# A transformer block's feed-forward part: source order on every engine, another load order for one weight sum, other final scalings on GpSimd

## The chip, the cores and the metric

The kernel runs on one core of a Trainium2 chip. Its time is the device time of one execution in microseconds (us); lower is better. Times come from runs of the whole kernel; everything about the inside of it comes from one profiled execution.

## The reference

One block of a model with a sequence of 512 tokens, width 2048 and a feed-forward width of 5632, everything in float32:

```python
u = rmsnorm(h, attn_norm_w)
z, xbc, dt_raw, q, kc, vc, ks, vs, kw, vw, gate_raw = split(u @ w_in)
y_ssd = ssd_mixer(...)            # a chunked state-space mixer
y_att = nsa_mixer(...)            # compressed, selected and window attention
h = h + concatenate([y_ssd, y_att]) @ w_out
v = rmsnorm(h, ffn_norm_w)
h = h + (silu(v @ w_gate) * (v @ w_up)) @ w_down
return rmsnorm(h, final_norm_w)
```

The change touches the last three lines: the feed-forward part and the final norm.

## The kernel before, in words

Up to about 900 us the kernel does the input projection, both mixers and the output projection. From there on it multiplies by the feed-forward weights. A product of two float32 matrices is made of three matmuls on halves of the numbers: each operand is split into a high part (ScalarE, `a_hi`, L117) and a low part (VectorE, `lo`, L120), and the matmuls are high x high, high x low (L1119, L1120) and low x high (L1121). The third matmul of each group of three is thus the first that needs the low part of a weight.

The gate and up products use a scheme with seven products in place of eight (Strassen and Winograd). A weight block of 1024 x 256 is cut into four quarters 11, 12, 21, 22; from them come the sums S1 = 21 + 22 and S3 = 21 + 11. The seven products are done in the order M1, M2, M6, M7, M5, M3, M4. M1 takes quarter 11, M2 quarter 12, M6 the quarter 11 with S1 added to it, M7 takes S3, M5 takes S1, M3 takes 12 with 11 added to it, M4 takes 22. One product is one *step* of 24 matmuls (128 x 256 each). The 22 *units* have two *sides* each, first gate, then up, so that a unit has 14 steps; the first and the last unit alternate their sides at the start (`pair_at_once`).

Weights come in buffers called `F`. The list `loads` sets the order of the blocks of a side: "11 12 S1 S3 22". A plain quarter is one load on SyncE's queue (L1065). S1 and S3 are two transfers: a load of one quarter (SyncE, L1065), and then a second transfer issued by GpSimd (L1067), which adds the other quarter onto it in the buffer and can only start when the first has landed. A side's five blocks pass through seven buffers, and a load is issued when a buffer comes free. Each weight block is then prepared for its step: where a sum is wanted, VectorE adds two buffers (`add`, L126, F<-F); ScalarE makes the high part three steps ahead of the product, VectorE the low part two steps ahead, both into buffers called `R`. VectorE and ScalarE also empty the results of the products (L126 with `ps`, L1288, L1291, L1278), VectorE multiplies (`mul`, L123) by the norm's row `rrow` and by the gate, and one transfer of 1792 KB per unit, issued by ScalarE (L1329), stores the unit's result in HBM (`g_d`).

From about 1950 us the down projection follows in the same scheme, in 36 visits of seven steps with 3 to 6 pairs of weight tiles each, and at the end the final norm: sums of squares, a power (`rst`, L1502, GpSimd), a row of factors, and sixteen multiplications of 128 x 512 in two halves, `lo_h` and `hi_h`, each followed by its stores (L1521).

The order in which the source emits all this is fixed by `run_step` and by a list of background tasks that advance by one after each group of three matmuls. In the kernel before, however, that isn't the order on the engines: the whole body is under a scheduler, which simulates the program and gives every engine (SyncE's and GpSimd's queues too) an order of its own.

Of the kernel before, what the change touches and what calls it, by code (L numbers as in the profile page):

```python
# [15 lines left out]
KD = D // 128  # L16
# [91 lines left out]
def body(ctx, tc, xT, w_in, w_out, w_gate, w_up, w_down, w1k, w1v, cols, rows, kst, out):  # L108
    nc = tc.nc
    act, dve, pool, pe = nc.scalar, nc.vector, nc.gpsimd, nc.tensor  # L110
    sch = Sched()
# [814 lines left out]
    order = [U_DTG]  # L926
# [113 lines left out]
    loads, items, steps = [], [], []  # L1040
# [46 lines left out]
    def prep(upto):  # L1087

        form(upto)
        while nxt["item"] <= min(upto, len(items) - 1):  # L1090
            i = nxt["item"]
            form(i + 1)
            b = items[i][0]
            hl[i].append(hl_place(b))
            assert hl[i][1] is not None, (i, hz.busy)
            lo(dve, hz.ap(hl[i][1], b.n), b.ap(), hz.ap(hl[i][0], b.n))
            b.read()
            nxt["item"] += 1
            advance()
# [8 lines left out]
    def run_step(s):  # L1108
        feed(s.i)
        if s.before:  # L1110
            s.before()
        prep(s.i + 2)
        n = s.blk.n
        ats = hl.pop(s.i)
        h, l = [hz.ap(a, n) for a in ats]
        p, q = s.psum()
        for k in range(s.blk.n):
            ah, al = s.rhs(k)
            pe.matmul(q, h[:, k, :], ah, start=(k == 0), stop=False)  # L1119
            pe.matmul(q, h[:, k, :], al, start=False, stop=False)  # L1120
            pe.matmul(q, l[:, k, :], ah, start=False, stop=(k == s.blk.n - 1))  # L1121
            sch.tick()
        for a in ats:
            hz.free(a, n)
        if s.after:
            s.after(p)
# [111 lines left out]
                     M5: (q["S1"], None), M3: (q["12"], q["11"]), M4: (q["22"], None)}  # L1238
        return q

    def add_loads(q, order="11 12 S1 S3 22"):
        loads.extend(q[a] for a in order.split())

    turn_ = {"n": 0}
# [5 lines left out]
    def banks(which=BANK):  # L1250
        got = {}

        def get(p):
            def g():
                b, h = which[p]
                if b not in got:
                    got[b] = bank()
                return got[b], got[b][:, 256 * h:256 * h + 256]
            return g
        return get  # L1260

    def v_rhs(p):
        a = V_OF[p]
        if a == 0:
            return lambda k: (P2["V0"][:, k, 0, :], P2["V0"][:, k, 1, :])
        if a < 3:
            return lambda k: (P2["VV"][:, a - 1, k, 0, :], P2["VV"][:, a - 1, k, 1, :])
        return lambda k: (P2["T"][a - 3][:, k, 0, :], P2["T"][a - 3][:, k, 1, :])
# [3 lines left out]
    def gu_after(u, side):  # L1272

        def after(pr):
            def ev(p):
                p1 = P2["HH"][:, 2 + side, :]
                if pr == M1:
                    act.activation(p1, p[:, lo_h], AF.Copy)  # L1278
                    return
                ct = P2["CT"].rearrange("p (s c a) t -> p s c (a t)", s=2, c=2)  # L1280
                c = ct[:, side].rearrange("p a t -> p (a t)")
                g = ct[:, 0].rearrange("p a t -> p (a t)")
                c11, c12, c21, c22 = [c[:, 256 * i:256 * i + 256] for i in range(4)]
                if pr == M6:
                    add(dve, c[:, 0:512].rearrange("p (a t) -> p a t", a=2), p.rearrange("p (a t) -> p a t", a=2),
                        p1[:, None, :].to_broadcast([128, 2, 256]))
                elif pr == M7:
                    dve.tensor_tensor(c21, p[:, lo_h], c12, ALU.subtract)  # L1288
                elif pr == M5:
                    add(dve, c22, p[:, lo_h], c21)  # L1290
                    dve.tensor_tensor(c12, c12, p[:, lo_h], ALU.subtract)  # L1291
                elif pr == M4:
                    add(dve, c[:, 256:768], p, c[:, 256:768])
                    if side == 0:
                        rr = rrow[:, None, :].to_broadcast([128, 2, 512])
                        c2 = ct[:, 0]
                        mul(dve, c2, c2, rr)
                        act.activation(g, g, AF.Silu)
                        sch.add(times_r(c2, rr))
                    else:  # L1300
                        mul(dve, c, c, g)
                        sch.add(g_forms(u))
            return ev
        return after
# [56 lines left out]
    def step_r3(ev):  # L1361
        def after(p):
            next(r3, None)
            ev(p)
        return after

    qs = {}
# [2 lines left out]
            qs[u, side] = quad(w[u], 0, 8)  # L1370
    def pair_at_once(u, before=None):

        loads.extend(qs[u, side][a] for a, side in (("11", 0), ("11", 1), ("12", 0), ("12", 1), ("S1", 0), ("S3", 0),
                                                    ("22", 0), ("S1", 1), ("S3", 1), ("22", 1)))
        seq = [(0, M1), (1, M1), (0, M2), (1, M2)] + [(i, p) for i in range(2) for p in SEQ[2:]]
        af = {0: gu_after(u, 0), 1: gu_after(u, 1)}
        bk = {0: banks(), 1: banks()}
        for n, (side, p) in enumerate(seq):
            ev = af[side](p)
            if u == 0 and n in (1, 2):  # L1380
                ev = step_r3(ev)
            b, plus = qs[u, side]["form"][p]
            s = Step(b, v_rhs(p), bk[side](p), after=ev, before=start_ff(n) if u == 0 and n < 3 else None, plus=plus)
            if u == NP - 1:
                done[V_SLOT.index(V_OF[p]) - GRING] = s.i
# [20 lines left out]
    def feed(i):  # L1406

        n = len(G)
        if n < NP and done.get(n - GRING, i) + 2 <= i:
            if n == NP - 1:  # L1410
                sch.run_until(("g", n))
            G[n] = P2["slot"][n % GRING][:, 0:7]
            nc.scalar.dma_start(f(G[n]), g_d[n])
        if "H0" not in P2 and len(G) > 0 and not any(fz.busy[NZ2:]):
            load_h(0)
            load_h(1)
            P2["H0"] = True
# [90 lines left out]
            pe.transpose(p[:, i * 128:(i + 1) * 128], rst[:, 4 + b + i:5 + b + i].to_broadcast([128, 128]), ident)  # L1508
        act.activation(rrow[:, t], p[:, 0:256], AF.Copy)

    def half_out(a, js):

        t = (lo_h, hi_h)[a]
        p = P2["rp", t.start // 128]
        for j in js:
            h = out_rows(j)[:, :, t]
            if j % 3 == 1:
                mul(pool, h, h, rrow[:, None, t].to_broadcast([128, 2, 256]))
            else:
                mul(dve, h, h, p[:, None, 0:256].to_broadcast([128, 2, 256]))  # L1520
            (nc.sync, nc.scalar)[j % 2].dma_start(out[2 * j:2 * j + 2, :, t].rearrange("c p t -> p c t"), h)  # L1521

    def d_end(j):
        order = [i for i in range(NJ) if i != j] + [j]

        def after(pr):
            def ev(p):
                H = P2["H"][j]
                q = p[:, 0:256]
                if pr == M1:  # L1530
                    d_add(j, M1, p, False, True)
                elif pr == M7:
                    add(dve, H[:, 3:5, :], p[:, None, lo_h].to_broadcast([128, 2, 256]), H[:, 3:5, :])
                elif pr == M5:
                    add(dve, H[:, 4, :], q, H[:, 4, :])
                    dve.tensor_tensor(H[:, 2, :], H[:, 2, :], q, ALU.subtract)
                    half_sum(lo_h)
                elif pr == M6:
                    add(dve, H[:, 0, :], q, H[:, 0, :])
                    add_x(j)  # L1540
                elif pr == M2:
                    add(dve, H[:, 1, :], q, H[:, 1, :])
                elif pr == M4:
                    add(dve, H[:, 3, :], q, H[:, 3, :])
                    half_sq(j, 0)
                elif pr == M3:
                    half_row(lo_h)
                    add(dve, H[:, 2, :], q, H[:, 2, :])
                    half_sq(j, 1)
                    half_out(0, order[:2])  # L1550
                    half_sum(hi_h)
                    half_out(0, order[2:5])
                    half_row(hi_h)
                    half_out(0, order[5:])
                    half_out(1, order)
            return ev
        return after

# [5 lines left out]
    for v, (j, a, b) in enumerate(visits):  # L1564
        q = quad(w_down[j], a, b, by_dma=False, s3_by_pool=v < 6)
# [9 lines left out]
        for n, p in enumerate(SEQ_END if end else SEQ_D):  # L1575
            blk, plus = q["form"][p]
            s = Step(blk, g_rhs(p, a), (lambda: (lambda t: (t, t[:, 0:256]))(bank())) if end else bk(p), after=af(p),
                     before=down_before(v) if n == 1 and 1 <= v < NJ - 1 else None, plus=plus)
        done.update((i, s.i) for i in range(a, b))

    def run_rest():
        pre_oa()
        for s in steps:
            run_step(s)
        sch.drain()
        for n in ("tt", "vv", "ws"):
            close_pool(n)

# [145 lines left out]
```

## Time and profile before

| | |
|---|---|
| three runs | 2479.65, 2484.35, 2484.87 us (median 2484.35) |
| the profiled execution | 2476.37 us, of which the span is 2473.9 us |
| mean granted TensorE clock | 0.952 |
| TensorE busy | 2259.7 us, 91% of the span |
| VectorE busy | 1802.3 us, 73% |
| ScalarE busy | 1096.1 us, 44% |
| GpSimd busy | 434.9 us, 18% |
| moved by DMA | 419.18 MB, mean 169 GB/s |

Busy time of TensorE includes the stretches in which its granted clock was half, so 91% busy doesn't say that 91% of the span was used at full speed. All stages share these means; the feed-forward part has to be read by windows of its own.

### The profile page before, as it was taken

What the parts mean: (1) busy time and instruction counts of PE and PEld (TensorE: products, weight loads), DVE (VectorE), ACT (ScalarE), POOL (GpSimd) and SP (SyncE); (2) the same over time, 40 slices, a digit from 0 to 9 for tenths busy, and PEclk for the clock granted to TensorE, in tenths of its full rate; (3) what the DMA queues carried; (4) which work ended last, traced back from release to release, by engine and by line L of the source; (5) the groups of instructions that cost most, each with busy time, mean ns of one, the idle gap of its engine ahead of it and who ended that gap; (6) DMA issues with size and microseconds to landing.
All of it is one profiled execution on the core that took longest, in us unless ns stands there. A gap on an engine that the chain in (4) does not pass through costs nothing. (4 is left out here: it accounts for less than half of the span.)

```text
span 2473.9 us, 39809 instructions
## 1 busy us (share of the span) xinstructions
PE 2259.7 (91%) x15376; PEld 2095.7 (85%) x15376; DVE 1802.3 (73%) x2916; ACT 1096.1 (44%) x1767; POOL 434.9 (18%) x441
## 2 busy tenths in 40 slices
PE   7999999999898999898988888788989889999987
PEld 5888888888687789888988888788989889999987
DVE  7699666777986677666676767576666777788886
ACT  4454446666765444333343333333333333333353
POOL 1011341332232330000000000000000121112122
PEclk9999999999999999998999899999989999899998
DMA  4222432222243767576767566666766857686865
GB/s 166 90 73 69 157 107 91 80 70 81 69 147 103 240 178 205 168 207 187 201 169 218 168 191 184 203 185 181 207 181 195 300 209 253 181 280 166 297 158 162
DMA packets 135469, 419.18 MB, mean 169 GB/s; under 512 B 16448, under 2 KB 22096, under 8 KB 129648
## 3 DMA queue, kind: packets, MB, share of 16 engines
q1 hardware_dynamic: 99840, 251.91, 31.1%
q0 software_dynamic: 25776, 77.70, 15.6%
q10 hardware_dynamic: 9664, 87.04, 8.7%
q8 instruction: 120, 1.97, 0.3%
q14 instruction: 69, 0.57, 0.1%
HBM read 354.45 MB, written 58.20 MB: 167 GB/s over the span
## 5 line engine op out<-in xcount | busy, mean ns | idle before, releaser
L117 ACT ACTIVATE R<-F 128x1024 fp32r<-128x1024 f32 (+4 forms) x576 | 512.1, 910 | 871.2 <-DVE F L126 421.7
L120 DVE TENSOR_TENSOR R<-F,R 128x1024 fp32r<-128x1024 f32 (+4 forms) x576 | 617.4, 1081 | 45.8 <-ACT R L117 31.2
L126 DVE TENSOR_TENSOR F<-F 128x1024 f32<-128x1024 f32 (+4 forms) x168 | 170.9, 1017 | 280.7 <-DMA F<-in_w_up 196.3
L224 PE MATMUL ps_g<-u_hi,whi 128*128 128x512 f32 x592 | 238.2, 402 | 0.0
L226 PE MATMUL ps_g<-u_hi,wlo 128*128 128x512 f32 x592 | 236.6, 400 | 0.0
L225 PE MATMUL ps_g<-u_lo,whi 128*128 128x512 f32 x592 | 236.2, 399 | 0.0
L1119 PE MATMUL ps_g<-T,R 128*128 128x256 f32 x704 | 201.5, 286 | 5.3 <-ACT R L117 5.3
L120 DVE TENSOR_TENSOR wlo<-wraw,whi 128x512 fp32r<-128x512 f32 x196 | 153.0, 783 | 70.9 <-ACT whi L117 70.0
L1119 PE MATMUL ps_s<-T,R 128*128 128x256 f32 x698 | 199.8, 286 | 4.1 <-ACT R L117 4.1
L1121 PE MATMUL ps_s<-T,R 128*128 128x256 f32 x698 | 200.1, 287 | 3.6 <-DVE R L120 3.6
L1121 PE MATMUL ps_g<-T,R 128*128 128x256 f32 x704 | 201.4, 286 | 1.0 <-DVE R L120 1.0
L1120 PE MATMUL ps_g<-T,R 128*128 128x256 f32 x704 | 200.8, 285 | 1.5 <-DVE T L120 1.5
L1119 PE MATMUL ps_t<-T,R 128*128 128x256 f32 x678 | 194.7, 287 | 6.3 <-ACT R L117 6.3
L1120 PE MATMUL ps_s<-T,R 128*128 128x256 f32 x698 | 199.2, 285 | 0.0
L1121 PE MATMUL ps_t<-T,R 128*128 128x256 f32 x678 | 194.9, 287 | 3.9 <-DVE R L120 3.9
L1120 PE MATMUL ps_t<-T,R 128*128 128x256 f32 x678 | 194.0, 286 | 0.0
L117 ACT ACTIVATE whi<-wraw 128x512 fp32r<-128x512 f32 x196 | 122.6, 626 | 145.2 <-PE ps_g L225 95.5
L1121 PE MATMUL ps_g<-VV,R 128*128 128x256 f32 x354 | 107.6, 304 | 42.3 <-DVE R L120 42.3
L1121 PE MATMUL ps_s<-VV,R 128*128 128x256 f32 x367 | 111.0, 303 | 37.6 <-DVE R L120 37.6
L1119 PEld LDWEIGHTS ps_g<-T,R 128*128 128x128 f32 x704 | 135.8, 193 | 6.6 <-ACT R L117 6.5
L1119 PEld LDWEIGHTS ps_s<-T,R 128*128 128x128 f32 x698 | 135.0, 193 | 4.8 <-ACT R L117 4.8
L1121 PEld LDWEIGHTS ps_s<-T,R 128*128 128x128 f32 x698 | 134.4, 193 | 5.1 <-DVE R L120 4.8
(406 smaller groups left out, 6495.0 us busy)
## 6 DMA issues: line engine op xcount, KB each, us to landing
F<-in_w_gate SPq DMA_DIRECT2D x110, 512.0 KB, 7.0
F<-in_w_up SPq DMA_DIRECT2D x110, 512.0 KB, 6.1
wraw<-in_w_in SPq DMA_DIRECT2D x164, 256.0 KB, 3.0
g_d<-F ACTq DMA_DIRECT2D x22, 1792.0 KB, 13.6
F<-in_w_gate POOLq DMA_DIRECT2D x44, 512.0 KB, 8.9
F<-in_w_up POOLq DMA_DIRECT2D x44, 512.0 KB, 11.2
F<-in_w_down SPq DMA_DIRECT2D x68, 320.0 KB, 3.7
T<-g_d ACTq DMA_DIRECT2D x12, 1792.0 KB, 10.9
```

What stands on the lines that cost most here:

```text
L117: act.activation(dst, src, AF.Copy, scale=scale)
L120: eng.tensor_tensor(dst, src, f(hi), ALU.subtract)
L126: eng.tensor_tensor(o, a, b, ALU.add)
L224: pe.matmul(p, hi_t[i][:, j, :], ah, start=(k == 0), stop=False)
L225: pe.matmul(p, hi_t[i][:, j, :], al, start=False, stop=False)
L226: pe.matmul(p, lo_t[i][:, j, :], ah, start=False, stop=(k == u.nk - 1))
L1119: pe.matmul(q, h[:, k, :], ah, start=(k == 0), stop=False)
L1120: pe.matmul(q, h[:, k, :], al, start=False, stop=False)
L1121: pe.matmul(q, l[:, k, :], ah, start=False, stop=(k == s.blk.n - 1))
```

## The change

It has three parts.

1. The steps after the first `KD` (those of the output projection) are put in a region of manual schedule. In it every engine runs in the order in which the source emits its instructions.
2. The load order of a side becomes "11 S1 12 S3 22": S1 is loaded second rather than third. In `pair_at_once` the up side's quarter 12 goes behind the gate side's S1.
3. In the final norm GpSimd takes the fourth and the seventh of each half's eight multiplications instead of the three with j % 3 == 1.

```diff
-    def add_loads(q, order="11 12 S1 S3 22"):
+    def add_loads(q, order="11 S1 12 S3 22"):
         loads.extend(q[a] for a in order.split())
...
-        loads.extend(qs[u, side][a] for a, side in (("11", 0), ("11", 1), ("12", 0), ("12", 1), ("S1", 0), ("S3", 0),
+        loads.extend(qs[u, side][a] for a, side in (("11", 0), ("11", 1), ("12", 0), ("S1", 0), ("12", 1), ("S3", 0),
                                                     ("22", 0), ("S1", 1), ("S3", 1), ("22", 1)))
...
-    def half_out(a, js):
+    def half_out(a, js, order):
...
-            if j % 3 == 1:
+            if order.index(j) in (3, 6):
                 mul(pool, h, h, rrow[:, None, t].to_broadcast([128, 2, 256]))
             else:
                 mul(dve, h, h, p[:, None, 0:256].to_broadcast([128, 2, 256]))
...
-                    half_out(0, order[:2])
+                    half_out(0, order[:2], order)
                     half_sum(hi_h)
-                    half_out(0, order[2:5])
+                    half_out(0, order[2:5], order)
                     half_row(hi_h)
-                    half_out(0, order[5:])
-                    half_out(1, order)
+                    half_out(0, order[5:], order)
+                    half_out(1, order, order)
...
-        for s in steps:
+        for s in steps[:KD]:
             run_step(s)
-        sch.drain()
+        with tc.manual_schedule():
+            for s in steps[KD:]:
+                run_step(s)
+            sch.drain()
```

Where instructions stand on the engines is seen in the built programs. On GpSimd, the two accumulating transfers of each side in the middle of the gate and up stage, before. `DMASW` are the semaphores of GpSimd's transfers, and each of these rows waits for the earlier use of its own one; `DMAHW` are those of the transfers of the other queues, here that of the load onto which the row accumulates. By the addresses in the program the first of each pair is S3's, the second S1's:

```order
L1067 DMA F<-in_w_gate 128x1024 [waits DMAHW6_49,DMASW6_49]
L1067 DMA F<-in_w_gate 128x1024 [waits DMAHW7_49,DMASW7_49]
L1067 DMA F<-in_w_up 128x1024 [waits DMAHW3_49,DMASW0_49]
L1067 DMA F<-in_w_up 128x1024 [waits DMAHW4_49,DMASW1_49]
L1067 DMA F<-in_w_gate 128x1024 [waits DMAHW1_49,DMASW2_49]
L1067 DMA F<-in_w_gate 128x1024 [waits DMAHW2_49,DMASW3_49]
```

The same rows of GpSimd after; here the first of each pair is S1's:

```order
L1067 DMA F<-in_w_gate 128x1024 [waits DMAHW4_49,DMASW6_49]
L1067 DMA F<-in_w_gate 128x1024 [waits DMAHW6_49,DMASW7_49]
L1067 DMA F<-in_w_up 128x1024 [waits DMAHW1_49,DMASW0_49]
L1067 DMA F<-in_w_up 128x1024 [waits DMAHW4_49,DMASW1_49]
L1067 DMA F<-in_w_gate 128x1024 [waits DMAHW7_49,DMASW2_49]
L1067 DMA F<-in_w_gate 128x1024 [waits DMAHW1_49,DMASW3_49]
```

Before, the two loads below a pair stand next to each other on SyncE (neighbouring semaphores); after, other transfers are issued between them.

On VectorE, the start of an up side before. The row with a `DMASW` wait and F<-F is the sum for M6; behind it stands a low part (R<-F,R), that of M2, and the row that waits for `DMASW0` further down is the low part of M7:

```order
L120 TENSOR_TENSOR R<-F,R 128x1024 [waits DMAHW5_49,PE_49,Activation_49]
L126 TENSOR_TENSOR F<-ps_g,F 128x256 [waits DVE_49]
L1291 TENSOR_TENSOR F<-F,ps_g 128x256
L126 TENSOR_TENSOR F<-F 128x1024 [waits DMASW1_49,DVE_49]
L120 TENSOR_TENSOR R<-F,R 128x1024 [waits DMAHW6_49,PE_49,Activation_49]
L126 TENSOR_TENSOR F<-F 128x1024 [waits DVE_49]
L126 TENSOR_TENSOR F<-ps_s,F 128x512 [waits PE_49]
L120 TENSOR_TENSOR R<-F,R 128x1024 [waits Activation_49]
L123 TENSOR_TENSOR F<-F,rrow 128x1024 [waits DVE_49]
L120 TENSOR_TENSOR R<-F,R 128x1024 [waits DMASW0_49,PE_49,Activation_49]
```

The same place after:

```order
L120 TENSOR_TENSOR R<-F,R 128x1024 [waits DMAHW4_49,Activation_49]
L126 TENSOR_TENSOR F<-F 128x1024 [waits DMASW0_49,DVE_49]
L120 TENSOR_TENSOR R<-F,R 128x1024 [waits DMAHW7_49,PE_49,Activation_49]
L126 TENSOR_TENSOR F<-ps_s,F 128x512 [waits PE_49]
L123 TENSOR_TENSOR F<-F,rrow 128x1024 [waits DVE_49]
L120 TENSOR_TENSOR R<-F,R 128x1024 [waits Activation_49]
L123 TENSOR_TENSOR F<-F,rrow 128x1024 [waits Activation_49]
L120 TENSOR_TENSOR R<-F,R 128x1024 [waits DMASW1_49,PE_49,Activation_49]
L126 TENSOR_TENSOR F<-F 128x1024
```

The sum for M6 now waits for the first of GpSimd's pair instead of the second, the low part of M7 for the second instead of the first, and the sum for M3 stands seven rows behind that for M6 instead of two.

At the end of the program, GpSimd's rows before:

```order
L1502 TENSOR_TENSOR rst<-rst,nhalf 128x2 [waits DVE_49]
L123 TENSOR_TENSOR F<-F,rrow 128x2x256 [waits DMASW6_49,Activation_49]
L123 TENSOR_TENSOR F<-F,rrow 128x2x256 x2
L1502 TENSOR_TENSOR rst<-rst,nhalf 128x2 [waits DVE_49]
L123 TENSOR_TENSOR F<-F,rrow 128x2x256 [waits Activation_49]
L123 TENSOR_TENSOR F<-F,rrow 128x2x256 x2
```

and after:

```order
L1502 TENSOR_TENSOR rst<-rst,nhalf 128x2 [waits DVE_49] x2
L123 TENSOR_TENSOR F<-F,rrow 128x2x256 [waits DMASW7_49,Activation_49]
L123 TENSOR_TENSOR F<-F,rrow 128x2x256
L123 TENSOR_TENSOR F<-F,rrow 128x2x256 [waits Activation_49]
L123 TENSOR_TENSOR F<-F,rrow 128x2x256
```

The second power now stands directly behind the first instead of behind three multiplications, and each half has two multiplications here instead of three.

## The prediction

> **What bounds the kernel now.** I first looked at the stretches of the span, to see which stage has something to lose. Columns: stretch, its length, then busy time (and instructions) of PE, PEld, DVE, ACT and POOL, the granted TensorE clock, the DMA engines' share, GB/s.
>
> ```profile
> 1100.00:1900.00 800.00, 700.75 (x5528) 696.47 (x5527) 534.59 (x612) 291.92 (x329) 57.13 (x66) 0.92 0.66 191
> ...
> 1900.00:2000.00 100.00, 84.35 (x644) 81.64 (x642) 69.08 (x91) 34.53 (x48) 13.52 (x10) 0.92 0.84 295
> 2000.00:2100.00 100.00, 96.58 (x798) 96.16 (x798) 80.48 (x110) 38.91 (x57) 21.49 (x14) 0.98 0.60 199
> 2100.00:2200.00 100.00, 95.11 (x741) 94.00 (x742) 80.69 (x114) 36.53 (x52) 20.47 (x17) 0.92 0.72 213
> 2200.00:2300.00 100.00, 97.69 (x805) 95.94 (x804) 81.07 (x115) 39.22 (x55) 19.11 (x15) 1.00 0.73 223
> ```
>
> The first row is the steady gate and up stage: TensorE is idle for 99 us of 800 and its clock is 0.92. The last row, in the down projection, shows that TensorE can be 98% busy at a clock of 1.00. Which wait ends last in the steady stage is told by its waits (total, times, longest) and by the matmuls that read `VV`, the operand of M2:
>
> ```profile
> ACT R L117 <- DVE F L126: 288.8, 30, 13.5
> DVE F L126 <- DMA F<-in_w_up: 162.8, 17, 10.2
> DVE F L126 <- DMA F<-in_w_gate: 54.4, 16, 4.9
> ```
>
> ```profile
>   DVE R L120: 99.2, 19
> ```
>
> All of TensorE's waits there are for a low part of M2, 99.2 us, and VectorE waits 162.8 us for a transfer into an up side's buffer. One unit's timeline joins the two (start, length, what, idle time before it):
>
> ```profile
> 1437.14 5.66 SPq L1065 DMA_DIRECT2D F<-in_w_up  x3
> ...
> 1441.22 0.86 POOL L1067 DMA_DIRECT2D F<-in_w_up  x1 [17.73 <-DMA F<-in_w_up]
> 1443.75 0.86 POOL L1067 DMA_DIRECT2D F<-in_w_up  x1 [1.67 <-DMA F<-in_w_up]
> ...
> 1445.12 0.33 ACTq L1329 DMA_DIRECT2D g_d<-F  x1
> ...
> 1448.67 0.41 DVE L1291 TENSOR_TENSOR F<-F,ps_g 128x256 f32<-128x256 f32 x1
> 1459.00 1.23 DVE L126 TENSOR_TENSOR F<-F 128x1024 f32<-128x1024 f32 x1 [9.92 <-DMA F<-in_w_up]
> 1460.15 1.22 DVE L120 TENSOR_TENSOR R<-F,R 128x1024 fp32r<-128x1024 f32 x1
> ...
> 1460.32 2.95 ACT L117 ACTIVATE R<-F 128x1024 fp32r<-128x1024 f32 x3 [12.93 <-DVE F L126]
> ...
> 1461.42 0.58 PE L1121 MATMUL ps_g<-VV,R 128*128 128x256 f32 x1 [6.26 <-DVE R L120]
> 1461.80 0.41 PE L1119 MATMUL ps_g<-VV,R 128*128 128x256 f32 x1
> 1462.01 0.41 PE L1120 MATMUL ps_g<-VV,R 128*128 128x256 f32 x1
> ```
>
> The second row of POOL is S1's accumulate. It is issued at 1443.75 and releases VectorE at 1459.00, 15.25 us later, with the `g_d` store in flight beside it. VectorE stands at M6's sum for 9.92 us; the low part of M2, which needs none of S1, is queued behind it, and TensorE waits 6.26 us for that. After the wait the matmuls start 0.21 us apart. Elsewhere they start 0.118 us apart, and a shorter wait brings the slow pace too:
>
> ```profile
> 1985.56 0.58 PE L1121 MATMUL ps_s<-V,R 128*128 128x256 f32 x1 [2.79 <-DVE R L120]
> ...
> 1990.42 0.39 PE L1121 MATMUL ps_t<-V,R 128*128 128x256 f32 x1
> ...
> 1991.01 0.28 PE L1119 MATMUL ps_t<-T,R 128*128 128x256 f32 x1
> ...
> 1993.96 0.28 PE L1119 MATMUL ps_g<-T,R 128*128 128x256 f32 x1
> ```
>
> (From 1991.01 to 1993.96 are 25 matmuls, 0.118 us each.) The length of a unit comes from its store:
>
> ```profile
> L1329 ACTq DMA_DIRECT2D g_d<-F x22: 326/326/338, 961.2 to 1983.1; - x22
> ...
> DMA to landing us min/median/max: 10.5/13.6/17.2
> ```
>
> (1983.1 - 961.2)/21 = 48.66 us per unit. Its 14 x 24 = 336 matmuls need 336 x 0.118 = 39.65. Of the 9.0 us between, 99.2/(800/48.66) = 6.0 are the wait and 3.0 the half clock behind it with small change.
>
> **The change part by part.**
>
> *S1 earlier, and really in the listed place.* Before, S1 was third in the list, but GpSimd's rows show S3 issued ahead of it. After, its load takes the buffer that is freed about nine steps before the sum that needs it; before it was five. Nine steps are 9 x 24 x 0.118 = 25.5 us. Before, from the first of the three load issues to the landing were 1459.0 - 1437.14 = 21.9 us; the three issues lie within 5.66 us and S1's is the second, so its own way took about 20. Both are below 25.5: S1's stall goes, worth up to 9.0 us a unit.
>
> What is late next is S3, which now takes the crowded place beside the store. Its product M7 comes eight steps after its load's issue: 8 x 24 x 0.118 = 22.7 us, less the high part (1.0 us) and the low part (1.22 us) ahead of it, 20.4 us. Its transfers there are bounded by the gate side of the same stage from below (its longest wait for DMA is 4.9 us against 10.2, so about 5 us shorter: 15 us, no stall) and by S1's 20.0 to 21.9 us from above. At a denser pace these may stretch: DMA share 0.66 at 48.66 us is 0.79 at 40.7; stretched in that ratio, 20.0 becomes 23.9, 3.5 us too late. I take the value nearest to the row of the same place, 20.0 to 21.9 against 20.4: about 0.8 us of stall, and with it a part of the half clock, 1.2 of the 3.0 us. A unit becomes 39.65 + 2.0 = 41.65, a gain of 7.0; over the 20 units in which the sides follow each other, **-140 us** (ends: -20 x 9.0 = -180 and, with 3.5 us of stall and 3.0 of clock, -20 x 2.5 = -50).
>
> [...]
>
> *Quarter 12 third instead of second.* Its high part is needed four steps after its issue, its product seven (19.9 us on TensorE). Plain loads in this stage have no row above S1's two in sequence, 20 us, and the plain half of that is 1441.22 - 1437.14 = 4.1 us: hidden, cost 0. If the cover goes, ScalarE stands at it, and with it every later high part.
>
> *Strict order in gate and up.* VectorE is busy 534.59/800 x 48.66 = 32.5 us a unit, 82% of 39.65; ScalarE 17.8, 45%. Both still fit, and the sum for M3 no longer stands ahead of an evacuation. At a unit's end a multiplication (1.22) and three subtractions (0.69, 0.42 and 0.42 in the rows of that time, 2.75 us in all) stand in one piece ahead of a low part that has a lead of two steps, 5.7 us: hidden. Unit 0 and the last unit alternate sides and their up side still loads S1 eighth of ten: no gain credited there, and in unit 0 the splitting of the operands (`T`), which VectorE now does in line, is ahead of low parts: **+5 us** (four `lo` of 1.22 us or longer; ends 0 and +10).
>
> *Strict order at the change of stages and in the down projection.* Before, the scheduler mixed the end of the last unit with the first visits; from 1900 to 2000 TensorE is busy 84.35 us at 0.92. In strict order this can be worse or better by what it loses now, 100 - 84.35 + 8 of clock = 24 us: I take **+4**. From 2000 on TensorE is above 95% busy with VectorE at 81 of 100; there are seven matmuls to one VectorE instruction (805 to 115). Strict order can win what the row 2100 to 2200 lacks against 2200 to 2300 (64 matmuls x 0.118 = 7.6 us) or lose as much again in each of four such stretches, 30 us: I take 0.
>
> *The final scalings.* The tail before:
>
> ```profile
> 2458.17 3.08 DVE L123 TENSOR_TENSOR F<-F,ps_v 128x512 f32<-128x512 f32 x5 [0.89 <-ACT rrow L1509]
> 2461.16 0.15 DVE L1501 TENSOR_SCALAR rst<-ps_m 128x2 f32<-128x2 f32 x1
> 2463.78 3.08 DVE L123 TENSOR_TENSOR F<-F,ps_m 128x512 f32<-128x512 f32 x5 [2.46 <-ACT rrow L1509]
> ...
> 2458.21 3.71 POOL L123 TENSOR_TENSOR F<-F,rrow 128x512 f32<-128x512 f32 x3 [1.07 <-ACT rrow L1509]
> 2461.89 0.69 POOL L1502 TENSOR_TENSOR rst<-rst,nhalf 128x2 f32<-128x2 f32 x1
> 2463.82 3.71 POOL L123 TENSOR_TENSOR F<-F,rrow 128x512 f32<-128x512 f32 x3 [1.24 <-ACT rrow L1509]
> ```
>
> The second power waits for three multiplications, until 2461.89; after, it stands ahead of them, and the second half starts when VectorE is through with six of the first, 6 x 0.62 + 0.15 = 3.9 after 2458.17: 2462.0 instead of 2463.8, 1.7 us. Each half's last multiplication on GpSimd falls from 3.71 to 2 x 1.24 = 2.5, VectorE's grows from 3.08 to 3.7, the same end. With earlier stores: **-3 us** (ends -4 and 0).
>
> Sum: -140 + 5 + 4 + 0 - 3 = -134 us. Against the profiled execution (2476.37) that is 2342. The three runs lie 3.3 to 8.5 us above that execution, and their median is 2484.35; against it the sum gives **2350 us**.
>
> **The rivals.**
>
> *The whole stall goes* (12 in 100). S3 lands in time like the gate side's transfers, and a unit is 39.65: -180 + 6, 2310 us. For it: most waits for in_w_gate were short. Against: the store lies beside S3.
>
> *S3 takes S1's place* (18 in 100). If the two transfers stretch with density, a unit of P us has a stall of 20.0 x 48.66/P - 20.4 and P is 39.65 + stall + 3.0. P settles at 44.25 with a stall of 1.6: -20 x 4.4 + 6, 2402 us; with 21.9 in place of 20.0 it settles at 45.6 with 3.0, 2429 us. VectorE would then stand at the low part of M7. For it: the 15.25 us beside the store. [...]
>
> *Strict order ruins the down projection* (6 in 100), the other side. Its 455 us have TensorE busy 95% now by a scheduler's order; with evacuations standing ahead of low parts on VectorE, TensorE and VectorE could take turns. At a share x the stage takes 0.95 x 455/x; it decides against the change when that is 134 us more, x below 0.73. At 0.70 it is +162, 2512 us. For it: VectorE's 81 of 100 leaves little room. Against: the low parts have two steps of lead.
>
> *The change doesn't do what it says* (4 in 100): the sum for M6 is late for another reason than its place, since the accumulate itself took 15 of the 20 us. A load issued ten us earlier would have to be slower by as much; then 2484 us.
>
> **How the numbers follow.** The forecast, 60 in 100: 2350, its own range 2315 to 2385 (the ends of the small terms and stalls of 0 to 2 us). The range 2300 to 2430 takes in the first rival and the second. A measurement of this kernel tells about 0.2% from no change. Faster: 0.60 + 0.12 + 0.17 = 0.89; slower: the third and a half of the fourth, 0.08; same 0.03.
>
> **What would show it.** Right: no wait of VectorE for in_w_up at L126 above 2 us, the `g_d` stores 41 to 42 us apart, the clock of the steady stage at 0.97 or more, DMA share near 0.78. The second rival shows as waits of ACT L117 or DVE L120 for DMA F<-in_w_up and stores 44 to 46 us apart. The third shows as PE under 90 in the hundred-us windows of the down projection. The power of the second half should start within 4 us of the first. The prediction is wrong above all if M2 waits again, or if the steady gain is given back behind the last store.

## The result and the profile after

The changed kernel takes 2321.31 us (median of four runs, 2318.81 to 2321.64) against 2482.0 us (the three runs of the table before and a fourth, 2471.6 to 2484.87): a ratio of 0.9357, 95% interval 0.9328 to 0.9387. The forecast was 2350 us, faster, with a range of 2300 to 2430.

Its profiled execution took 2321.24 us, span 2319.3. The stretches after, with the same columns as before:

```profile
1000.00:1780.00 780.00, 779.52 (x6545) 779.31 (x6545) 637.45 (x717) 347.28 (x390) 65.66 (x76) 1.00 0.79 232
1780.00:1818.00 38.00, 25.01 (x183) 24.30 (x182) 23.59 (x31) 11.02 (x16) 6.30 (x6) 0.85 0.77 271
1818.00:1868.00 50.00, 44.30 (x348) 43.77 (x348) 39.69 (x58) 18.07 (x29) 11.35 (x6) 0.94 0.65 250
1868.00:1968.00 100.00, 91.82 (x747) 91.22 (x746) 72.48 (x107) 35.88 (x53) 18.30 (x14) 0.95 0.72 239
1968.00:2068.00 100.00, 95.55 (x786) 95.04 (x785) 84.58 (x124) 38.66 (x57) 19.19 (x16) 0.97 0.77 240
```

For 780 us in the gate and up stage TensorE is idle for half a microsecond and has its full clock; before, it was idle 99 of 800 us at 0.92. In this stage TensorE is now what bounds the time. What is left of waits lies in the last unit (second row) and in the down projection (last three). The units' stores and their landing:

```profile
L1329 ACTq DMA_DIRECT2D g_d<-F x22: 326/326/356, 963.9 to 1820.1; - x22
...
DMA to landing us min/median/max: 6.7/6.7/19.1
```

A steady unit takes 40.0 us, where the matmuls alone need 39.65. The store lands in 6.7 us (median) instead of 13.6. The span is 154.6 us shorter, and the starts of the stores divide this: up to the first store nothing is won (+2.7 us), from first to last the 21 intervals give -165.7, from the last store to the end of the last weight product the down projection takes 481.6 us instead of 472.3 (+9.3), and the tail behind that product 17.6 instead of 18.6 (-1.0). The timeline of one store, in the place in which S1 stood before:

```profile
1324.09 0.33 ACTq L1329 DMA_DIRECT2D g_d<-F  x1
...
1325.27 2.90 SPq L1065 DMA_DIRECT2D F<-in_w_up  x3
...
1333.99 0.86 POOL L1067 DMA_DIRECT2D F<-in_w_up  x1 [14.29 <-DMA F<-in_w_up]
1337.80 0.86 POOL L1067 DMA_DIRECT2D F<-in_w_gate  x1 [2.95 <-DMA F<-in_w_gate]
```

Only one accumulating transfer of this side (S3's, 1333.99) now lies behind the store; S1's was issued 15 us earlier, at 1318.8, and lands as the store starts. The store itself lands at 1331.1, before S3's is issued. The up side's accumulating transfers land after 5.5 us here (median), so that S3 is there some 14 us after the load at 1325.27, where the prediction had taken 20 to 22 against a need of 20.4.

### The profile page after: what moved, and what is told of

Its sections match the earlier page's. It is cut to its first block, busy times and chain, and to the rows that moved or that the text cites. A ratio compares the mean times of both kernels' runs of the same rounds, so it can differ in the third digit from the quotient of the medians.

```text
span 2319.3 us, 39808 instructions
## 1 busy us (share of the span) xinstructions
PE 2215.3 (96%) x15376; PEld 2057.3 (89%) x15376; DVE 1803.0 (78%) x2918; ACT 1098.1 (47%) x1767; POOL 430.9 (19%) x439
## 5 line engine op out<-in xcount | busy, mean ns | idle before, releaser
L120 DVE TENSOR_TENSOR R<-F,R 128x1024 fp32r<-128x1024 f32 (+4 forms) x576 | 610.6, 1067 | 37.8 <-ACT R L117 28.2
L1121 PE MATMUL ps_s<-T,R 128*128 128x256 f32 x698 | 203.0, 291 | 23.0 <-DVE R L120 23.0
L1119 PE MATMUL ps_s<-T,R 128*128 128x256 f32 x698 | 201.2, 288 | 0.0
L1120 PE MATMUL ps_s<-T,R 128*128 128x256 f32 x698 | 201.1, 288 | 0.0
L1121 PE MATMUL ps_t<-T,R 128*128 128x256 f32 x678 | 192.6, 284 | 0.4 <-DVE R L120 0.4
L1120 PE MATMUL ps_t<-T,R 128*128 128x256 f32 x678 | 192.0, 283 | 0.0
L1119 PE MATMUL ps_t<-T,R 128*128 128x256 f32 x678 | 192.0, 283 | 0.0
L1121 PEld LDWEIGHTS ps_s<-T,R 128*128 128x128 f32 x698 | 136.7, 196 | 25.3 <-DVE R L120 25.1
L1119 PEld LDWEIGHTS ps_s<-T,R 128*128 128x128 f32 x698 | 136.7, 196 | 0.0
L1120 PEld LDWEIGHTS ps_s<-T,R 128*128 128x128 f32 x698 | 136.6, 196 | 0.0
L1121 PEld LDWEIGHTS ps_g<-T,R 128*128 128x128 f32 x704 | 133.8, 190 | 3.0 <-DVE R L120 2.9
L1119 PEld LDWEIGHTS ps_g<-T,R 128*128 128x128 f32 x704 | 133.6, 190 | 1.7 <-ACT R L117 1.3
```

Source lines behind the costliest of these rows:

```text
L120: eng.tensor_tensor(dst, src, f(hi), ALU.subtract)
```

## The experiments

All are timed against the kernel before on the chip on which they ran. These chips differ: the kernel before has a median of 2480 us on one and 2499 on two others, so kernels of different sets are compared by ratios, and kernels of one set by times. Ratios don't carry from chip to chip exactly either: the kernel after has 0.9357 above and 0.9291 when timed again below, at nearly the same time, 2321 and 2322 us. A difference of under 0.7% between sets therefore tells nothing.

**Each part alone.** The manual region with the old lists and old scalings (the edit is against the kernel after):

```diff
-    def add_loads(q, order="11 S1 12 S3 22"):
+    def add_loads(q, order="11 12 S1 S3 22"):
...
-                                    (("11", 0), ("11", 1), ("12", 0), ("S1", 0), ("12", 1), ("S3", 0),
+                                    (("11", 0), ("11", 1), ("12", 0), ("12", 1), ("S1", 0), ("S3", 0),
...
-            if order.index(j) in (3, 6):
+            if j % 3 == 1:
```

> The manual region alone: old load order, old last scalings. Source order puts S1's transfers ahead of S3's on both queues, but S1 is still third in the list, so that its load is issued about 5 steps (14.2 us) before the sum that needs it. Theory (the place of S1's load decides): its way is 13.8 us in the quiet place of the profile after and 20 us beside the store, so the stall shrinks but stays, 1 to 5 us a unit with half clock behind it: 2360 to 2430 us, stores 41.5 to 45 us apart. Rival (only the order of the two accumulating transfers counts, or the strict order as such): no wait for in_w_up, stores 40 us apart, 2325 us.

Measured: 2459.96 us, ratio 0.9928 (0.9904 to 0.9952). The direction is the theory's, the size isn't: 2360 to 2430 was expected. The other half, the two lists alone in the kernel before, without a manual region:

> The load order alone: the scheduler still sets the order on every engine, old last scalings. In the built program S1's accumulate now stands ahead of S3's, but the two loads are still neighbours. Theory (place of S1's load decides): S1 comes at the time at which S3 came before, about 10 us sooner than before; the wait of 6 us at M6's sum goes for the most part, 2340 to 2400 us. Rival (strict order is what brings the gain): the stall stays at 5 to 6 us a unit, about 2480 us.

Measured: 2312.55 us, ratio 0.933 (0.930 to 0.9359): the whole gain. Again on another chip, beside the kernel after:

> The kernel after once more, beside the next two on the same chip, since the chips differ by more than the kernels do. Theory (with the new load order the strict order costs some 10 us, in the last unit and the down projection): ratio to before 0.935 to 0.938. Rival (strict order costs nothing): equal to the next kernel's ratio within 0.002.

> The load order alone, under the scheduler, beside the kernel after. Theory: ratio 0.003 to 0.006 below the kernel after's (7 to 14 us). Rival: within 0.002 of it.

Measured: the kernel after 2322.34 us, ratio 0.9291 (0.9267 to 0.9316); the load order alone 2309.64 us, 0.9253 (0.9223 to 0.9284). So the load order alone brings all of it. It has the lowest median of the study; the medians lie 12.7 us apart and the profiled spans 16.1 (2322.1 and 2306.0 us), so that the region of manual schedule, with the new scalings, seems to cost 13 to 16 us on top of it. That isn't clear of the noise: the intervals overlap, and one of the five runs of the load order alone took 2323.75 us. The steady stage of the load order alone, and what GpSimd issues there in a unit:

```profile
1000.00:1760.00 760.00, 760.00 (x6384) 760.00 (x6383) 621.66 (x703) 345.00 (x381) 63.93 (x74) 1.00 0.79 231
```

```profile
1425.42 0.86 POOL L1067 DMA_DIRECT2D F<-in_w_up  x1 [9.87 <-DMA F<-in_w_up]
1433.00 0.86 POOL L1067 DMA_DIRECT2D F<-in_w_up  x1 [6.72 <-DMA F<-in_w_up]
```

The two transfers stand 7.6 us apart under the scheduler, 2.5 us in the kernel before. The scheduler itself puts S1 first once the list does; no manual region is needed for it.

**S1 behind S3, in strict order.**

```diff
-    def add_loads(q, order="11 S1 12 S3 22"):
+    def add_loads(q, order="11 12 S3 S1 22"):
```

> The kernel after with the load order 11 12 S3 S1 22 for the steady units: strict order, but S3's transfers ahead of S1's, as the scheduler had them before. Theory: S1 is the second of two accumulating transfers that start within 3 us of each other beside the store; the stall of about 6 us a unit returns with the half clock, stores 47 to 49 us apart, 2450 to 2480 us. Rival (the strict order on VectorE hides it): under 2350 us.

Measured: 2595.23 us, ratio 1.0474 (1.0443 to 1.0504): worse than before, and outside what was expected. TensorE waits twice a unit, 6 us on the up side and 2 on the gate side, and the stores stand (2080.4 - 965.5)/21 = 53.1 us apart. By the source, S1's load now waits for one buffer more than in the kernel before, where the scheduler had only put it behind S3 in the queues. The region alone, above, is in strict order too and has S1 third: there TensorE waits 3.7 us a unit on the up side and not at all on the gate side, here 6.2 and 2.2. One place later in the list thus costs about one step of 24 matmuls (2.8 us at full pace) on either side. In strict order the wait on the up side goes 0, 3.7, 6.2 us with S1 second, third and fourth.

**Does the store lengthen S1's way?** In the manual region with the old lists the store was issued later, once by 22 us (out of the way) and once by 9 us (beside the two accumulating transfers, as in the kernel before):

```diff
-        yield 6
+        yield 68      # the other one: 31
         nc.scalar.dma_start(g_d[u], f(sg))
```

> The manual region with the old load order, and each unit's store to HBM (1792 KB) issued some 22 us later, out of the way of the up side's loads. In manual_only S1's way from load issue to landing was 17 us on the up side with the store just ahead of it, its load alone 6.8 to 8.5 us against 3.5 to 5 on the gate side, and TensorE waited 3.8 us a unit. Theory (the store sets the length of that way): the way falls to 14 to 15 us, TensorE's wait to 0 to 1.5 us a unit, 2370 to 2410 us. Rival (two accumulating transfers at once are what is long, the store counts little): the way stays above 16 us, 2445 to 2470 us.

> The manual region with the old load order and each unit's store issued some 9 us later than in source order, so that it is in flight beside the up side's two accumulating transfers, as it was in the kernel before. Theory (the store and two accumulating transfers at once make the 15 us): S1's accumulate takes 13 to 15 us instead of 8.7, its way 18 to 20 us, TensorE's wait 5 to 6.5 us instead of 3.8; ratio to before 1.00 to 1.02 against 0.993. Rival (the store counts little): accumulate under 11 us, ratio 0.985 to 0.997.

Times: 2451.92 us, 0.982 (0.9793 to 0.9847), with the store out of the way, and 2486.58 us, 0.9942 (0.9917 to 0.9966), with it beside. Both lie in the range of their rival; what the transfers do is another matter. The transfers in the steady stage (KB each, median us to landing), first the region alone, then the store beside, then out of the way:

```profile
g_d<-F ACTq DMA_DIRECT2D x12, 1792.0 KB, 6.7
F<-in_w_up POOLq DMA_DIRECT2D x26, 512.0 KB, 8.6
```

```profile
g_d<-F ACTq DMA_DIRECT2D x13, 1792.0 KB, 12.5
F<-in_w_up POOLq DMA_DIRECT2D x26, 512.0 KB, 12.9
```

```profile
g_d<-F ACTq DMA_DIRECT2D x13, 1792.0 KB, 10.6
F<-in_w_up POOLq DMA_DIRECT2D x26, 512.0 KB, 9.3
```

Beside two accumulating transfers the store takes 12.5 us instead of 6.7, and they take 12.9 instead of 8.6; in the kernel after, one at a time, they take 5.5 (median of the up side). That is the collision of the kernel before, made again. TensorE's wait went up with it, 57.6/12 = 4.8 us against 48.4/13 = 3.7. The signs are the theory's, the sizes fall short of it.

Moving the store away did not bring the expected 0 to 1.5 us a unit. TensorE's waits at M2 in 600 us of the steady stage, for the region alone and then for the store out of the way:

```profile
  DVE R L120: 48.4, 13
```

```profile
  DVE R L120: 51.8, 26
```

They are twice as many and half as long, 2.0 us: the store now lies beside the gate side's transfers, and M2 waits on both sides. VectorE's waits for M6's sum tell the sides apart (total, times, longest), again for the region alone and then for the store out of the way:

```profile
DVE F L126 <- DMA F<-in_w_up: 105.6, 13, 8.9
DVE F L126 <- DMA F<-in_w_gate: 39.8, 13, 4.3
```

```profile
DVE F L126 <- DMA F<-in_w_gate: 85.5, 12, 8.4
DVE F L126 <- DMA F<-in_w_up: 72.7, 13, 6.3
```

On the up side, which the store left, a wait falls from 8.1 to 5.6 us; on the gate side, to which it came, one rises from 3.1 to 7.1. From the issue of its load to its landing S1 takes 13.3 us on the up side instead of 15.7 (medians), and TensorE waits there for about 1.3 us a unit instead of 3.7; on the gate side it takes 15.1 us instead of 13.0, and TensorE waits for 2.7 us instead of not at all. So the theory holds for the side that the store leaves, and what was won there was lost on the other. Of the 3.7 us the store accounts for about two thirds; the rest stays without it, at 5 steps of lead. The steady stage as a whole won next to nothing: the stores are (1976.4 - 987.2)/21 = 47.1 us apart against (1949.2 - 958.1)/21 = 47.2, although TensorE's mean clock over the profiled run is 0.97 instead of 0.96. Why the better clock doesn't show there is open, and so is the 1% between the two ratios, which come from two chips.

**The down projection under the scheduler.**

```diff
         with tc.manual_schedule():
-            for s in steps[KD:]:
+            for s in steps[KD:KD + 14 * NP]:
                 run_step(s)
-            sch.drain()
+        for s in steps[KD + 14 * NP:]:
+            run_step(s)
+        sch.drain()
```

> The kernel after with the down projection left to the scheduler; the gate and up steps stay in the manual region. From the last store to TensorE's end were 472 us before and 482 us after. Theory A (strict order costs the down projection about 9 us): 472 us again, 2312 us in all. Theory B (the five waits of 2 to 8 us there come from stored units' loads of 1792 KB that share the DMA engines with the weights, whatever the order): 478 to 484 us, 2317 to 2325 us.

Measured: 2321.79 us (2310.85 to 2328.2), ratio 0.9376 (0.9342 to 0.9409). The time lies in theory B's range. In the profile, the fastest of its runs, the down projection took 469.6 us from the last store to the end of the last weight product, as theory A has it, but the last unit grew by 5 us, and the median doesn't tell it from the kernel after. Inconclusive.

**S1 sooner in the last unit.** What stops TensorE at the end of the gate and up stage in the kernel after:

```profile
1784.91 0.86 POOL L1067 DMA_DIRECT2D F<-in_w_up  x1 [3.65 <-DMA F<-in_w_up]
...
1788.62 1.23 DVE L126 TENSOR_TENSOR F<-F 128x1024 f32<-128x1024 f32 x1 [12.96 <-DMA F<-in_w_up]
1789.76 1.22 DVE L120 TENSOR_TENSOR R<-F,R 128x1024 fp32r<-128x1024 f32 x1
...
1791.03 0.58 PE L1121 MATMUL ps_s<-T,R 128*128 128x256 f32 x1 [9.90 <-DVE R L120]
```

It is the old chain once more, in the unit in which S1 is still the eighth load. The edit makes it the seventh:

```diff
-    ("S3", 0), ("22", 0), ("S1", 1), ("S3", 1), ("22", 1)
+    ("S3", 0), ("S1", 1), ("22", 0), ("S3", 1), ("22", 1)
```

> The kernel after, with the up side's S1 of the first and last unit loaded before the gate side's 22 instead of behind it (seventh of ten instead of eighth). Theory (the waits of 4.2 us at 937 and 9.9 us at 1791 are the sum for M6 of the up side waiting for an S1 that is loaded too late, the same mechanism as in the steady units before): both go, with their half clock -14 to -20 us, 2301 to 2308 us. Rival (the next item, S3 or 22, is late instead): 2315 to 2325 us.

> The same edit on the kernel whose down projection is left to the scheduler. Theory (the two gains add): 2290 to 2300 us by the profile. Rival (the scheduler was hiding the late S1 of the last unit in part, or the down projection loses again what the last unit wins): 2305 to 2320 us.

> The load order alone, under the scheduler, with the same edit. There TensorE had no wait over 1.5 us before 1775, and the last unit took 9.7 us longer than a steady one, 4.9 of it a wait for a high part. Theory (that wait is not S1's): no change beyond 5 us, 2305 to 2315 us. Rival (S1 is late there too and the scheduler fills the time with other work): 2295 to 2303 us.

> The kernel after with the up side's S1 of the first and last unit loaded seventh, beside the kernel after. On another chip both of its waits at those places were gone and the last store came 11 us sooner, but the whole did not show it. Theory (that chip's down projection was slower): ratio 0.003 to 0.006 below the kernel after's, like the load order alone. Rival (the down projection gives the 11 us back, its waits moving with the start): within 0.002 of the kernel after.

Measured: 2336.75 us, 0.9364 (0.9341 to 0.9386) on the kernel after; 2332.22, 0.9341 (0.9315 to 0.9367) with the down projection scheduled; 2325.28, 0.9317 (0.9292 to 0.9342) on the load order alone. Beside the kernel after on one chip it was 2339.84 us against 2322.34, 0.9366 (0.9342 to 0.9391) against 0.9291 (0.9267 to 0.9316): slower, where theory and rival had faster or the same. The first three times lie above theory and rival alike, and for the load order alone the new ratio lies between its two old ones, 0.933 and 0.9253: no gain is shown in any of them. Beside the kernel after both old waits are gone (the last store starts at 1807.7 instead of 1818.2), though a new one of 3.6 us stands at 1783, where ScalarE waits for the next up block, as the rival had it. The down projection gives back more than was won, 510 us instead of 486. Two equal stretches of it, 350 to 450 us behind the last store, in the kernel after and then in this one:

```profile
2168.20:2218.20 50.00, 46.09 (x381) 45.27 (x380) 36.30 (x55) 20.78 (x32) 9.79 (x8) 1.00 0.63 181
2218.20:2268.20 50.00, 44.98 (x349) 43.27 (x349) 39.71 (x61) 24.74 (x39) 12.99 (x12) 0.97 0.74 175
```

```profile
2157.70:2207.70 50.00, 40.66 (x302) 39.97 (x302) 33.22 (x49) 17.82 (x25) 9.04 (x8) 0.90 0.63 190
2207.70:2257.70 50.00, 40.54 (x301) 38.95 (x300) 31.11 (x52) 20.24 (x33) 11.60 (x12) 0.90 0.58 132
```

There are 127 matmuls fewer in these 100 us, with the DMA engines less busy: weights are asked for later. The buffers of the down projection have five sizes and are taken from one pool, so that one swap of two loads shifts where all later blocks lie and when one fits. Counted in matmuls of the traces, 14 of the down projection's 174 plain weight loads are issued one to three steps (of 24 matmuls) later than in the kernel after, half of them among the last fifty, and two earlier; between the two profiles of the kernel after itself no load moves by more than 0.7 of a step. That this is the cause was not tested by itself.

## Why the prediction was right, and where its terms were off

The forecast of 2350 us was right in its direction and in what moves the time, and 29 us too high; the measured 2321.31 lies closer to the first rival's 2310.

*What bounds the kernel.* Right: S1's accumulating transfer holds M6's sum, M2's low part stands behind it, TensorE waits. With the list alone, under the scheduler, the wait and the half clock went from the steady stage (busy 760.00 of 760 us at 1.00).

*S1 earlier, -140 us.* Right in mechanism, too small. From the first store to the last but one the unit went from 48.59 to 40.08 us, 8.5 a unit and 170 over twenty. The term that was off is the price of S3 in the crowded place: 0.8 us of stall and 1.2 of clock were taken from S1's 20 to 21.9 us there. Measured, S3 lands 13 to 16 us after its load's issue, and TensorE never waits for it. Two things were wrong with the 20 to 21.9. The upper end runs from the first of the three loads; S1's own is the second, at 1439.41, and from its issue S1 took 18.6 to 19.7 us in this stage, below the need of 20.4. And it was the price of a crowd: S1's accumulating transfer ran beside the store, three plain loads (issued from 1442.47 to 1446.29) and, for 3.6 of its 15.2 us, S3's. After, S1's transfer and the store have landed before S3's is issued; a price read beside a collision was used after the collision was gone. So the steady stage went by the first rival (the whole stall goes, 39.65), to which 12 in 100 were given. The second rival, S3 in S1's place, didn't happen. One sign of it was seen, waits of ScalarE for S3 (17 in 780 us, at most 1.9 us), but the lead of three steps hides them, and the stores are 40 us apart and not 44 to 46. Nor did the accumulating transfers stretch with density, as that rival had it: at a DMA share of 0.79 instead of 0.66 they take 5.5 us (median of the up side) where they took 11.1, with VectorE busy 637 of 780 us, 82%, against 67% before.

*"And really in the listed place".* Wrong as a reason for the region: the scheduler with the new list puts S1 first too.

*Quarter 12, 0.* Right in cost, but not because its load is out of the way: ScalarE waits for quarter 12 on the up side, 16 times in the 780 us, for 2.6 to 4.6 us. In one unit (the first row waits for 12, loaded behind the store from 1285.25 on, the second for S3):

```profile
1292.14 1.06 ACT L117 ACTIVATE R<-F 128x1024 fp32r<-128x1024 f32 x1 [2.57 <-DMA F<-in_w_up]
...
1300.71 1.06 ACT L117 ACTIVATE R<-F 128x1024 fp32r<-128x1024 f32 x1 [0.43 <-DMA F<-in_w_up]
```

The high part is made three steps ahead, and TensorE does not wait for it.

*Strict order in gate and up, +5; change of stages, +4; down projection, 0.* By the stores: up to the first store +0.5 us from the end of the output projection, in the last unit +4.4, in the down projection +9.3 where 0 was taken (ends -7.6 and +30), +14 in sum. But the store is a late mark. It starts 14.0 us behind the first unit's matmuls before and 7.0 after, and this hides what that unit lost. Counted in matmuls, of which each profile has all 11472, the first unit takes 56.2 us instead of 48.7, the next twenty 168.6 less in sum, the last 53.3 instead of 53.4 (before, the scheduler mixed it with the first visits), and the down projection 5.3 more. So the +5 for the first unit was about right, at +7.5; there are two waits in it, the second for the late S1 of its up side:

```profile
911.28 0.58 PE L1121 MATMUL ps_g<-VV,R 128*128 128x256 f32 x1 [3.63 <-DVE R L120]
...
937.10 0.58 PE L1121 MATMUL ps_s<-T,R 128*128 128x256 f32 x1 [4.15 <-DVE R L120]
```

The load order alone has 47.7 us in the first unit and 50.3 in the last, which is most of the 15 us between the first pair of profiles. In the down projection it has 490.4 us (489.8 on the other chip), the kernel after 490.9 (496.6) and the kernel before 485.6: what was lost there is not shown to be the strict order's. One of the waits in the down projection:

```profile
1947.89 1.52 POOL L126 TENSOR_TENSOR F<-F 128x640 f32<-128x640 f32 x1 [25.25 <-DMA F<-in_w_down]
...
1949.44 0.83 DVE L126 TENSOR_TENSOR F<-F 128x640 f32<-128x640 f32 x1 [9.85 <-POOL F L126]
...
1951.06 0.58 PE L1121 MATMUL ps_s<-VV,R 128*128 128x256 f32 x1 [7.90 <-DVE R L120]
```

GpSimd's sum waits for a weight, VectorE for GpSimd, TensorE for VectorE. The transfers issued from 1922 to 1938 say why the weight is late:

```profile
T<-g_d ACTq DMA_DIRECT2D x2, 1792.0 KB, 16.7
F<-in_w_down SPq DMA_DIRECT2D x7, 320.0 KB, 12.9
V<-g_d ACTq DMA_DIRECT2D x1, 1792.0 KB, 8.3
VV<-g_d ACTq DMA_DIRECT2D x1, 1792.0 KB, 14.1
```

Four stored units come back at once, and a weight block takes 12.9 us; the median of such loads is 3.7 over the whole run before and 5.1 after. The third rival, strict order ruining this stage, didn't happen: from 1868 to 2268 TensorE is busy 92 to 100 of each 100 us.

*The final scalings, -3.* Too large: the tail fell by 1.0 us, and the region with the old scalings has 17.8 us against 17.6, so the new choice of multiplications is worth 0.2. The second power starts 3.3 us behind the last weight product instead of 6.5, but 5.25 us behind the first power (at 2299.76), not within 4:

```profile
2304.78 0.15 DVE L1501 TENSOR_SCALAR rst<-ps_m 128x2 f32<-128x2 f32 x1
...
2305.01 0.70 POOL L1502 TENSOR_TENSOR rst<-rst,nhalf 128x2 f32<-128x2 f32 x1 [4.55 <-DVE rst L1501]
...
2307.24 3.67 DVE L123 TENSOR_TENSOR F<-F,ps_m 128x512 f32<-128x512 f32 x6
...
2308.20 6.51 ACTq L1521 DMA_DIRECT2D outT<-F  x6
```

The multiplications end at 2310.9, 9.2 us behind the last weight product instead of 12.2: they did win the forecast 3 us. But the issues of the last stores run to 2314.7 and the span to 2319.3: the tail ends by its stores, not by the multiplications.

*Clock for a short stall.* The prediction took 1.2 us of clock for a stall of 0.8. Its row for a shorter wait, 2.79 us at 1985.56, is no clean case: two shorter waits, of 0.29 and 0.85 us, end within the 5 us before it. No stall was left in the steady stage of the kernel after to decide it. In the kernel before, two waits of the size, 0.82 us (ended at 2338.90) and 0.83 us (at 2381.43), had a clock of 1.00 in the 7.8 us from their start on; in the kernel with S3 first (below) a wait of 1.81 us had 1.00 around it and one of 2.51 us 0.83. These waits don't bear out 1.2 us for a stall of 0.8.

The medians lie 160.7 us apart where 134 were forecast; between the profiled executions it was 155: -170 instead of -140, +14 instead of +9, -1 instead of -3 (by the stores), and +2 before the feed-forward part. The signs of the forecast that were met are the clock (1.00), the DMA share (0.79) and no wait of VectorE for an up block at a sum; the stores came closer together than forecast, 40.0 us instead of 41 to 42.

## What to carry to other kernels

Where an engine stands at a sum whose weight comes in two dependent transfers, with other work behind the sum in its order (VectorE stood 9.92 us here), give that weight the earliest buffer in the load list; nine steps of lead instead of five (23 us in the trace of the kernel after) removed a wait and its half clock, 8.5 us of each 48.6. A transfer time read beside a collision is the price of that collision (11.1 us before, 5.5 after): ask whether the change also dissolves it, and see what waits where the other transfer is moved to (here one wait fell from 8.1 to 5.6 us and another rose from 3.1 to 7.1). Try the reordering without the rewrite of the schedule: here the list alone brought the whole gain. And an edit of a load list can be felt hundreds of microseconds later: one swap that removed two waits made the kernel slower, 2339.84 us against 2322.34.

## What the runs showed of the hardware that was not expected

In the records of the two traces, of the kernel before and of the kernel after, the granted clock of TensorE is either whole or half. Between 900 us and the final norm half clock stands there 28 times before and nine times after, for 3.41 to 10.24 us each. Three waits of TensorE in the kernel with S3 first, and the stretches around them (clock in the third column from the end):

```profile
1544.63 0.39 PE L1121 MATMUL ps_t<-VV,R 128*128 128x256 f32 x1 [1.81 <-DVE R L120]
...
1573.19 0.58 PE L1121 MATMUL ps_s<-VV,R 128*128 128x256 f32 x1 [6.18 <-DVE R L120]
...
1597.70 0.58 PE L1121 MATMUL ps_g<-VV,R 128*128 128x256 f32 x1 [2.51 <-DVE R L120]
```

```profile
1542.00:1549.00 7.00, 3.94 (x32) 3.53 (x30) 6.65 (x8) 3.59 (x5) 0.00 (x0) 1.00 0.01 2
...
1595.20:1605.00 9.80, 7.24 (x46) 7.03 (x47) 9.57 (x12) 5.11 (x7) 0.00 (x0) 0.83 0.00 0
1571.00:1583.00 12.00, 9.81 (x67) 9.81 (x68) 11.52 (x11) 6.29 (x7) 0.47 (x1) 0.74 0.25 75
```

Around a wait of 1.81 us the clock was 1.00; around one of 2.51 us it was 0.83, which is 0.17 x 9.8 x 2 = 3.3 us at half clock, and around one of 6.18 us 0.74, which is 0.26 x 12 x 2 = 6.2 us. Why it was half beside the one and whole beside the other, no run here shows.
